# Heads of 64 rows against heads of 32 + 32 rows: the q and k layout of a dilated attention branch

## The chip, the cores and the metric

The kernel runs on one core of a Trainium2 chip. The metric is the time of one execution in microseconds on the device. Three runs of the kernel before gave 249.78, 249.79 and 250.01 us; the median is 249.79 us. The core has five engines that run side by side: TensorE (PE, matmuls; its weight loads are shown apart as PEld), VectorE (DVE), ScalarE (ACT), GpSimd (POOL) and SyncE (SP), and DMA queues.

## The reference, cut to what matters

Two layers run over 256 positions of width 1024. Each layer normalises its input, projects it by one large weight, runs three branches on the parts of the projection (dilated attention with 8 heads, a gated linear recurrence, stick-breaking attention with 4 heads), gates them, and projects back. Only the dilated branch is touched here.

```python
def apply_partial_rope(x, cos, sin):          # x: one head of 64; ROPE_DIM = 16
    x1, x2 = x[..., :8], x[..., 8:16]
    return concatenate([x1*c - x2*s, x2*c + x1*s, x[..., 16:]], -1)   # 48 of 64 are left as they are

qa, ka = rope(a_q), rope(a_k)                 # 8 heads of 64
s = einsum('bhqd,bhkd->bhqk', qa / 8, ka)     # with masks of three dilated windows
p = softmax(s); y = p @ v
```

Of a head's 64 numbers, 16 are rotated by a table of sines and cosines, and 48 pass. The scores of a head are one product over its 64 numbers.

## The kernel before, in words

All matrix work is exact fp32, either as three products of split numbers (high and low halves of the weights, `whi` and `wlo`, and of the activations, `xh` and `xl`), or as plain fp32 matmuls. ACT makes `whi` (line 109) and DVE makes `wlo` (line 110) for each chunk of weights that SP loads; up to four chunks are held.

The order of TensorE's instructions is written out by hand (`manual_schedule` for PE). The order on DVE and ACT is found by the framework's scheduler when the program is built, so an edit on these engines can move other instructions too.

`proj_b` (line 314) computes 256 columns of the projection, transposed: columns on the partitions, two blocks `b` of 128 columns, 256 positions each. The 256 columns of one chunk of q or k are four heads; a block holds two heads, 64 rows each. In layer 0 the result stays in one PSUM bank (`pp`), since it must still be scaled by a row `rb` of the normalisation; in layer 1 each block is added up by ACT (`low`, line 335) and DVE (line 337) into an SBUF tile.

`rotate` (lines 476 to 484) is four DVE instructions over 128 rows and both blocks, 512 columns each: a shuffle of rows (481), a product with the cosines (482; the table has ones in the 48 rows that pass), a product of the shuffled copy with the sines (483; zeros there), and a sum (484). In layer 0 the table `rp0` already carries the factor `rb` (line 596).

`dil_scores` (line 489) computes the scores of four heads. For two heads at a time it takes two PSUM banks (`s`, from a pool of four) and issues four matmuls (line 497) in the order: first 128 queries of head one, of head two, then the other 128 queries of each. Head one lies on rows 0 to 63 of the array, head two on rows 64 to 127. The trace shows each fp32 matmul as two records. DVE then adds the mask and takes the minimum (504), ACT takes the exponential, and TensorE transposes the result (463) for the product with the values (427).

There are four such score blocks: `second()` runs inside the projection of the second q chunk, `third()` inside the projection of the gate, in each of two layers. `rotate` is called eight times. `sb_scores` (443) has the same form as `dil_scores` and is not changed. `lru_gates` (557) uses 64 by 64 pieces of the array.

Of the kernel before, what the change touches and what calls it, by code (L numbers as in the profile page):

```python
# [13 lines left out]
ALU = mybir.AluOpType  # L14

P = 128
S = 256
# [3 lines left out]
NK = D // P  # L21
HD = 64
# [18 lines left out]
SHUF = list(range(8, 16)) + list(range(0, 8)) + list(range(16, 32))  # L41

CH_AV, CH_CV, CH_CQ, CH_CK, CH_BX, CH_CG, CH_BG, CH_AG, CH_O = 0, 2, 3, 4, 7, 10, 11, 12, 14
CH_AQ, CH_AK = (5, 8), (6, 9)
# [4 lines left out]
def trunk_kernel(ctx: ExitStack, tc: tile.TileContext, x, first_x, first, wpack, prm_d, gatew, gains, consts, rope, out):  # L49
    nc = tc.nc  # L50
    act, dve, pe, gps = nc.scalar, nc.vector, nc.tensor, nc.gpsimd
# [7 lines left out]
    at = ctx.enter_context(tc.tile_pool(name="at", bufs=4, space=bass.MemoryType.PSUM))  # L59
    yp = ctx.enter_context(tc.tile_pool(name="yp", bufs=1, space=bass.MemoryType.PSUM))  # L60

    def bank(pool, tag):
        return pool.tile([P, 512], F32, name=tag, tag=tag)

    def scr(w):
        return wk.tile([P, 512], F32, name="scr", tag="scr", bufs=SCR)[:, 0:w]
# [20 lines left out]
    def v2(a, n=2):  # L87
        return a.rearrange("p (b t) -> p b t", b=n)
# [28 lines left out]
    def ask(l, c, ahead=AHEAD):  # L117
        last = order.index((l, c)) + ahead
        while pending and order.index(pending[0]) <= last:
            i = pending.pop(0)  # L120
            ready[i] = load_chunk(*i)

    def weights(l, c, ahead=AHEAD):
        ask(l, c, ahead)
        return ready.pop((l, c))
# [16 lines left out]
    for k in range(NK):  # L142
# [24 lines left out]
        for (i, (a, b)), (ps, base, c0, c1) in seq:  # L167
            for t in range(NT):
                pe.matmul(ps[t][:, c0 - base:c1 - base], a[:, k, t * P:(t + 1) * P], b[:, c0:c1],  # L169
                          start=k == 0 and i == 0 and c0 == base, stop=k == NK - 1 and i == 2,  # L170
# [35 lines left out]
    def mm3(ps, lhs, rhs, ks, first, last):  # L206
        lh, ll = lhs
        rh, rl = rhs
        seq = [(a, b, k) for a, b in ((lh, rh), (lh, rl), (ll, rh)) for k in ks]
        for i, (a, b, k) in enumerate(seq):  # L210
            pe.matmul(ps, a(k), b(k), start=first and i == 0, stop=last and i == len(seq) - 1)  # L211
# [80 lines left out]
    rp = cst.tile([P, 2, S], F32, name="rp")  # L292
    rp0 = cst.tile([P, 2, S], F32, name="rp0")
    rb = cst.tile([P, S], F32, name="rb")
    gn = cst.tile([P, D], F32, name="gn", tag="gn")

    for l in range(L):
# [16 lines left out]
        def proj_b(c, mid=None, to=None, sc=1.0):  # L314
            pair = c in PAIRED[l]
            hi, lo = [a.rearrange("p (k c) -> p k c", c=256) for a in weights(l, c, AHEAD - 1 if mid else AHEAD)]
            if pair:
                flat = None if to is not None else scr(512)
                to = v2(flat) if to is None else to
            else:  # L320
                flat = bank(pp, "pp")
            for b in range(2):
                cs = slice(b * P, b * P + P)
                if pair:
                    ps = bank(pp, "pp")
                    seq = [(0, k) for k in range(NK - 1)] + [(1, k) for k in range(NK)] + [(0, NK - 1)]
                    for i, (is_lo, k) in enumerate(seq):
                        if is_lo:
                            pe.matmul(ps[:, 0:S], lo[:, k, cs], xh[:, k, :], start=False, stop=False,  # L329
                                      skip_group_check=True)  # L330
                        else:
                            pe.matmul(ps, hi[:, k, cs], xx[:, k].rearrange("p h t -> p (h t)"), start=i == 0,  # L332
                                      stop=i == len(seq) - 1, skip_group_check=True)
                    low = wk.tile([P, S], F32, name="low", tag="low", bufs=2)
                    act.activation(low, ps[:, S:2 * S], AF.Copy, scale=sc)  # L335
                    if sc == 1.0:
                        dve.tensor_add(to[:, b, :], ps[:, 0:S], low)
                    else:
                        dve.scalar_tensor_tensor(to[:, b, :], ps[:, 0:S], sc, low, ALU.mult, ALU.add)
                else:  # L340
                    mm3(flat[:, b * 256:(b + 1) * 256], [lambda k, a=a: a[:, k, cs] for a in (hi, lo)],
                        [lambda k, a=a: a[:, k, :] for a in (xh, xl)], range(NK), True, True)
                if b == 0 and mid:
                    mid()
                    ask(l, c)
            return flat

        def proj_to(dst, c, mid=None, sc=1.0):
            if l > 0 and c in PAIRED[l]:
                proj_b(c, mid, dst, sc)  # L350
            else:
                scaled(dst, proj_b(c, mid), sc)

# [30 lines left out]
        for t in range(NT):  # L384
            sc = rstd0[t] if l == 0 else 1.0
# [32 lines left out]
        def head(h):  # L418
            return slice((h % 2) * HD, (h % 2) * HD + HD), h // 2, slice(h * HD, (h + 1) * HD)
# [13 lines left out]
        zs, sw = {}, {}  # L433
        halves = ((0, slice(0, 128)), (1, slice(128, 384)))
# [38 lines left out]
            parts[2] = a[:, 768:1024], b[:, 0:128]  # L473
            return parts

        def rotate(ps, tiles, h0, tag):
            dst = tiles[h0] = sb.tile([P, 2, S], F32, name=tag, tag=tag)
            rt_ = rp0 if l == 0 else rp
            cc, ss = [rt_[:, i:i + 1, :].broadcast_to([P, 2, S]) for i in range(2)]
            sw = scr(512)  # L480
            dve.stream_shuffle(sw, ps, SHUF)
            dve.tensor_mul(dst, v2(ps), cc)
            dve.tensor_mul(v2(sw), v2(sw), ss)
            dve.tensor_add(dst, dst, v2(sw))

        qT, kT = {}, {}
        prob = {}

        def dil_scores(h0):
            sps = {}  # L490
            for p in (h0, h0 + 2):
                for h in (p, p + 1):
                    sps[h] = bank(at, "s")
                for t, cs in halves:
                    for h in (p, p + 1):
                        hr, hb, _ = head(h - h0)
                        pe.matmul(sps[h][:, cs], qT[h0][hr, hb, t * P:(t + 1) * P], kT[h0][hr, hb, 0:(t + 1) * P],  # L497
                                  start=True, stop=True)
            shifted = {}
            for h in range(h0, h0 + 4):  # L500
                xs = scr(384)
                mn = wk.tile([P, 2], F32, name="mn", tag="mn", bufs=4)
                for t, cs in halves:
                    dve.tensor_tensor_reduce(xs[:, cs], sps[h][:, cs], nmask[:, cs], -0.125, 3e38,  # L504
                                             ALU.add, ALU.min, mn[:, t:t + 1])
                shifted[h] = xs, mn
            return shifted
# [86 lines left out]
        if l == 0:  # L594
            for i in range(2):
                dve.tensor_mul(rp0[:, i, :], rp[:, i, :], rb)
        rotate(proj_b(CH_AQ[0], sb_scores), qT, 0, "q0")
        rotate(proj_b(CH_AK[0]), kT, 0, "k0")
        sw_t, sw_heads = turned_tile()
        conv(lambda: turned(sw, 0, (0,), sw_t))  # L600
        turned(sw, 0, (1, 2), sw_t)
# [3 lines left out]
            table(LN_EXP)  # L605
            dil_softmax(dil_scores(0))

        rotate(proj_b(CH_AQ[1], second), qT, 4, "q1")
        rotate(proj_b(CH_AK[1]), kT, 4, "k1")
        table(SIGM)  # L610
        cg_ps = proj_b(CH_CG)
        pts = dil_transposes(0)
# [15 lines left out]
        ps = proj_b(CH_AG)  # L628
# [26 lines left out]
        for t in range(NT):  # L655
# [3 lines left out]
            for n2 in range(2):  # L659
                cs = slice(n2 * 512, n2 * 512 + 512)  # L660
# [5 lines left out]
                for c0, c1 in parts:  # L666
                    c = slice(n2 * 512 + c0, n2 * 512 + c1)
# [19 lines left out]
def _rope_table():  # L687
    f = np.float32
    pos = np.arange(S, dtype=f)
    inv = f(500000.0) ** (-np.arange(0, 16, 2, dtype=f) / f(16))  # L690
    ang = (pos[:, None] * inv[None, :]).astype(f)
    cos, sin = np.cos(ang).T, np.sin(ang).T
    tab = np.zeros((P, 2, S), f)
    tab[:, 0] = 1.0
    for h in range(2):
        r = h * HD
        tab[r:r + 8, 0] = tab[r + 8:r + 16, 0] = cos
        tab[r:r + 8, 1] = -sin
        tab[r + 8:r + 16, 1] = sin
    return tab  # L700


def _pack_weights(w_in, w_out):
    wp = np.empty((L, NCH, P, 2048), np.float32)
    narrow = ((CH_CV, 3072), (CH_BX, 2048), (CH_BG, 2304), (CH_AG, 1536), (CH_AG + 1, 1792), (CH_CG, 3328),
              (CH_CQ, 2560), (CH_CK, 2816), (CH_AQ[0], 0), (CH_AQ[1], 256), (CH_AK[0], 512), (CH_AK[1], 768))
    yk = (4, 5, 6, 7, 0, 1, 2, 3)
    for l in range(L):
        wi = w_in[l].reshape(NK, P, 3584)
        for h in range(2):  # L710
            wp[l, CH_AV + h] = wi[4 * h:4 * h + 4, :, 1024:1536].transpose(1, 0, 2).reshape(P, 2048)
        for c, col in narrow:
            wp[l, c] = wi[:, :, col:col + 256].transpose(1, 0, 2).reshape(P, 2048)
        wo = w_out[l].reshape(NK, P, D)
        for h in range(2):
            for n in range(2):
                blk = np.stack([wo[k, :, n * 512:n * 512 + 512] for k in yk[4 * h:4 * h + 4]])
                wp[l, CH_O + 2 * h + n] = blk.transpose(1, 0, 2).reshape(P, 2048)
    return wp
# [56 lines left out]
```

## Time and profile before

| what | value |
|---|---|
| median of three runs | 249.79 us |
| the profiled execution | 248.82 us |
| its span, first to last instruction | 246.7 us |
| TensorE busy | 239.0 us, 97% |
| TensorE weight loads busy | 212.1 us, 86% |
| DVE busy | 196.5 us, 80% |
| ACT busy | 167.2 us, 68% |
| mean granted TensorE clock | 0.996 |

The profiled execution lies 0.97 us below the median of the runs; 2.1 us of it lie outside the span. Shares are means over the whole span; whether an engine that is 80% busy matters is read from who waits for it. Matmul records overlap, so the distance from one start to the next, not the length of a record, says what a matmul takes of TensorE's time.

### The profile page before, as it was taken

The page shows a single profiled execution, that of the slowest core. Times are in us where ns is not written, and L with a number is a line of the kernel's source. Part 1 is how long each engine was busy: PE and PEld are TensorE (multiplying, and loading weights), DVE is VectorE, ACT ScalarE, POOL GpSimd, SP SyncE. Part 2 cuts the span into 40 slices and gives each one's busy share as a digit, 9 for nine tenths or more (in the row PEclk, how much of TensorE's full clock was granted, in tenths as well). Part 3 has the DMA queues.
Part 4 walks back from the last instruction along what each step waited for, and adds up shares of the span by engine and source line. Part 5 has one row for each costly group of instructions (what it writes and reads, how often), then busy time and mean ns, then how long its engine had stood idle before and what let it go on. Part 6 is the DMA issues. An engine that isn't in the chain of part 4 may idle for free.

```text
span 246.7 us, 4531 instructions
## 1 busy us (share of the span) xinstructions
PE 239.0 (97%) x1657; PEld 212.1 (86%) x1657; DVE 196.5 (80%) x442; ACT 167.2 (68%) x360; POOL 12.1 (5%) x45
## 2 busy tenths in 40 slices
PE   8999999999999999999999999999999999999990
PEld 4889999999998899878889988889889889987870
DVE  3885699999999799985792766999999987985253
ACT  3778989735947499964662885865498649992142
POOL 0037000001000000000100000000010000000000
PEclk9999999999999999999999999999999999999998
DMA  6989889268447741277157486605553672000022
GB/s 201 404 292 403 342 288 333 96 215 268 134 157 255 258 117 56 85 240 284 74 189 232 142 268 243 200 7 165 161 157 119 197 262 98 0 0 3 0 85 85
DMA packets 13173, 43.89 MB, mean 178 GB/s; under 512 B 1632, under 2 KB 2144, under 8 KB 13152
## 3 DMA queue, kind: packets, MB, share of 16 engines
q1 hardware_dynamic: 12384, 42.30, 51.1%
q10 hardware_dynamic: 576, 0.79, 0.9%
q0 software_dynamic: 192, 0.52, 0.7%
q8 instruction: 13, 0.21, 0.4%
q14 instruction: 8, 0.07, 0.1%
HBM read 42.03 MB, written 1.05 MB: 175 GB/s over the span
## 4 chain that ended last, share of the span: by engine, by line
PE 94%; DMA 2%; DVE 1%; ACT 1%; SPq 0%; issue 0%; ACTq 0%
PE pp L211 51%; PE pp L332 11%; PE s L211 9%; PE pp L329 5%; PE s L169 4%; PE s L463 3%; PE s L497 2%; PE y L427 2%; DMA st<-first 2%; PE pp L169 2%; PE s L443 1%; PE pp L427 1%; PE s L557 1%; PE s L259 1%; DVE xres L668 0%; ACT scr L242 0%
## 5 line engine op out<-in xcount | busy, mean ns | idle before, releaser
L110 DVE TENSOR_TENSOR wlo<-st,whi 128x512 fp32r<-128x512 f32 x132 | 84.1, 683 | 12.8 <-ACT whi L109 12.5
L109 ACT ACTIVATE whi<-st 128x512 fp32r<-128x512 f32 x132 | 73.9, 629 | 28.0 <-PE pp L211 11.8
L211 PE MATMUL pp<-xx,whi 128*128 128x256 f32 x480 | 63.3, 285 | 0.0
L211 PEld LDWEIGHTS pp<-xx,whi 128*128 128x128 f32 x480 | 59.7, 191 | 1.4 <-issue 1.3
L211 PE MATMUL pp<-xx,wlo 128*128 128x256 f32 x240 | 33.7, 283 | 0.0
L211 PEld LDWEIGHTS pp<-xx,wlo 128*128 128x128 f32 x240 | 30.9, 192 | 0.0
L332 PE MATMUL pp<-xx,whi 128*128 128x512 f32 x112 | 29.3, 396 | 0.0
L332 PEld LDWEIGHTS pp<-xx,whi 128*128 128x128 f32 x112 | 20.1, 189 | 4.1 <-ACT scr L83 0.3
L77 ACT ACT_TABLE_LOAD x13 | 16.7, 1283 | 1.9 <-PEq L769 1.7
L83 ACT ACTIVATE pr<-scr,mn 128x128 f32<-128x128 f32 (+1 forms) x32 | 14.1, 442 | 5.2 <-DVE mn L504 5.2
L329 PEld LDWEIGHTS pp<-xx,wlo 128*128 128x128 f32 x112 | 15.3, 190 | 1.1
L329 PE MATMUL pp<-xx,wlo 128*128 128x256 f32 x112 | 15.6, 282 | 0.0
L211 PE MATMUL pp<-whi,yh 128*128 128x512 f32 x48 | 14.5, 403 | 0.0
L211 PE MATMUL pp<-wlo,yh 128*128 128x512 f32 x48 | 14.0, 393 | 0.0
L211 PE MATMUL pp<-whi,yl 128*128 128x512 f32 x48 | 14.0, 393 | 0.0
L335 ACT ACTIVATE low<-pp 128x256 f32<-128x256 f32 x14 | 5.3, 382 | 9.1 <-PE pp L332 6.8
L211 PEld LDWEIGHTS pp<-wlo,yh 128*128 128x128 f32 x48 | 9.0, 188 | 2.1
L211 PEld LDWEIGHTS pp<-whi,yl 128*128 128x128 f32 x48 | 9.0, 188 | 2.0
L211 PEld LDWEIGHTS pp<-whi,yh 128*128 128x128 f32 x48 | 8.6, 188 | 2.0 <-issue 0.3
L169 PE MATMUL s<-whi,xx 128*128 128x512 f32 (+1 forms) x36 | 10.2, 404 | 0.1
L415 ACT ACTIVATE yh<-scr 128x512 fp32r<-128x512 f32 x8 | 5.0, 631 | 7.7 <-DVE scr L413 7.6
L504 DVE CUSTOM_DVE_ANT_0 scr<-s,con 128x128 f32<-128x128 f32 (+1 forms) x32 | 9.2, 351 | 0.0
(165 smaller groups left out, 355.2 us busy)
## 6 DMA issues: line engine op xcount, KB each, us to landing
st<-w_pack SPq DMA_DIRECT2D x66, 512.0 KB, 5.4
st<-first SPq DMA_DIRECT2D x7, 512.0 KB, 6.2
xres<-x_in SPq DMA_DIRECT2D x2, 512.0 KB, 8.1
gw_t<-gate_w SPq DMA_DIRECT2D x2, 256.0 KB, 6.9
gn<-gains SPq DMA_DIRECT2D x1, 512.0 KB, 6.7
xs<-xc POOLq DMA_DIRECT2D x4, 128.0 KB, 3.7
gf<-gains SPq DMA_DIRECT2D x1, 512.0 KB, 6.8
out<-scr SPq DMA_DIRECT2D x2, 256.0 KB, 2.1
```

The lines of the kernel that those rows point to most:

```text
L77: load = act.preload_act_table_set(name)
L83: i = dep(act.activation(*a, **k), loaded["load"])
L109: split[l, c] = act.activation(hi[:, ws], st[:, ss], AF.Copy)
L110: dve.tensor_sub(lo[:, ws], st[:, ss], hi[:, ws].bitcast(F32))
L169: pe.matmul(ps[t][:, c0 - base:c1 - base], a[:, k, t * P:(t + 1) * P], b[:, c0:c1], start=k == 0 and i == 0 and c0 == base, stop=k == NK - ...
L211: pe.matmul(ps, a(k), b(k), start=first and i == 0, stop=last and i == len(seq) - 1)
L329: pe.matmul(ps[:, 0:S], lo[:, k, cs], xh[:, k, :], start=False, stop=False, skip_group_check=True)
L332: pe.matmul(ps, hi[:, k, cs], xx[:, k].rearrange("p h t -> p (h t)"), start=i == 0, stop=i == len(seq) - 1, skip_group_check=True)
L335: act.activation(low, ps[:, S:2 * S], AF.Copy, scale=sc)
L427: pe.matmul(y[hr, p * 128 + o:p * 128 + 256], vt[:, s0, hs], wts[i][s0], start=s0 == 0, stop=s0 == 1)
L463: pe.transpose(tp[:, i * P:(i + 1) * P], tiles[h0 + h][:, j * P:(j + 1) * P], ident)
L504: dve.tensor_tensor_reduce(xs[:, cs], sps[h][:, cs], nmask[:, cs], -0.125, 3e38, ALU.add, ALU.min, mn[:, t:t + 1])
```

## The change

The rows of q and k are laid out anew by the order of the weights' columns (`_pack_weights`): block 0 holds the first 32 numbers of each of four heads (the 16 that are rotated and 16 more), block 1 the other 32 of each. A head is then 32 rows of block 0 and the same 32 rows of block 1.

`rotate` becomes `rotated`. Shuffle, two products and the sum run over block 0 alone, 256 columns instead of 512. In layer 0 block 1 still needs its scale, a fifth instruction of 256 columns; in layer 1 the projection writes block 1 straight into the tile. In `dil_scores` all four banks are taken first, and each head's product over 64 rows becomes two products over 32 rows that accumulate in the bank: 16 matmuls in a block instead of 8, four heads in turn on four row groups.

```diff
-                to = v2(flat) if to is None else to
+                to = [v2(flat)[:, b, :] for b in range(2)] if to is None else to
...
-                        dve.tensor_add(to[:, b, :], ps[:, 0:S], low)
+                        dve.tensor_add(to[b], ps[:, 0:S], low)
...
-        def rotate(ps, tiles, h0, tag):
+        def rotated(c, tiles, h0, tag, mid=None):
             dst = tiles[h0] = sb.tile([P, 2, S], F32, name=tag, tag=tag)
-            rt_ = rp0 if l == 0 else rp
-            cc, ss = [rt_[:, i:i + 1, :].broadcast_to([P, 2, S]) for i in range(2)]
-            sw = scr(512)
-            dve.stream_shuffle(sw, ps, SHUF)
-            dve.tensor_mul(dst, v2(ps), cc)
-            dve.tensor_mul(v2(sw), v2(sw), ss)
-            dve.tensor_add(dst, dst, v2(sw))
+            tab_ = rp0 if l == 0 else rp
+            if l > 0:
+                src = scr(S)
+                proj_b(c, mid, [src, dst[:, 1, :]])
+            else:
+                ps = proj_b(c, mid)
+                src = ps[:, 0:S]
+            sh = scr(S)
+            dve.stream_shuffle(sh, src, SHUF)
+            dve.tensor_mul(dst[:, 0, :], src, tab_[:, 0, :])
+            dve.tensor_mul(sh, sh, tab_[:, 1, :])
+            dve.tensor_add(dst[:, 0, :], dst[:, 0, :], sh)
+            if l == 0:
+                dve.tensor_mul(dst[:, 1, :], ps[:, S:2 * S], rb)
...
         def dil_scores(h0):
             sps = {}
-            for p in (h0, h0 + 2):
-                for h in (p, p + 1):
-                    sps[h] = bank(at, "s")
-                for t, cs in halves:
-                    for h in (p, p + 1):
-                        hr, hb, _ = head(h - h0)
-                        pe.matmul(sps[h][:, cs], qT[h0][hr, hb, t * P:(t + 1) * P], kT[h0][hr, hb, 0:(t + 1) * P],
-                                  start=True, stop=True)
+            for h in range(h0, h0 + 4):
+                sps[h] = bank(at, "s")
+            for t, cs in halves:
+                for part in range(2):
+                    for h in range(h0, h0 + 4):
+                        hr = slice(32 * (h - h0), 32 * (h - h0) + 32)
+                        pe.matmul(sps[h][:, cs], qT[h0][hr, part, t * P:(t + 1) * P],
+                                  kT[h0][hr, part, 0:(t + 1) * P], start=part == 0, stop=part == 1)
...
-        rotate(proj_b(CH_AQ[0], sb_scores), qT, 0, "q0")
-        rotate(proj_b(CH_AK[0]), kT, 0, "k0")
+        rotated(CH_AQ[0], qT, 0, "q0", sb_scores)
+        rotated(CH_AK[0], kT, 0, "k0")
...
-    for h in range(2):
-        r = h * HD
+    for r in range(0, P, 32):
         tab[r:r + 8, 0] = tab[r + 8:r + 16, 0] = cos
...
-            wp[l, c] = wi[:, :, col:col + 256].transpose(1, 0, 2).reshape(P, 2048)
+            blk = wi[:, :, col:col + 256]
+            if c in CH_AQ + CH_AK:
+                blk = blk.reshape(NK, P, 4, 2, 32).transpose(0, 1, 3, 2, 4).reshape(NK, P, 256)
+            wp[l, c] = blk.transpose(1, 0, 2).reshape(P, 2048)
```

On TensorE, at the second score block of layer 0, the program before has these instructions (s is a PSUM bank, k1 and q1 the rotated tiles; the semaphores that an instruction waits for stand in brackets):

```order
L497 MATMUL s_1156<-k1_998,q1_929 128x128 [waits DVE_49,PE_49]
L497 MATMUL s_1157<-k1_998,q1_929 128x128 [waits PE_49]
L497 MATMUL s_1156<-k1_998,q1_929 128x256
L497 MATMUL s_1157<-k1_998,q1_929 128x256
L497 MATMUL s_1162<-k1_998,q1_929 128x128 [waits PE_49,Activation_49]
L497 MATMUL s_1163<-k1_998,q1_929 128x128 [waits PE_49,Activation_49]
L497 MATMUL s_1162<-k1_998,q1_929 128x256
L497 MATMUL s_1163<-k1_998,q1_929 128x256
```

In the changed program the block begins so, and goes on with eight of 128x256 that wait for nothing:

```order
L504 MATMUL s_1168<-k1_946,q1_811 128x128 [waits DVE_49,PE_49]
L504 MATMUL s_1169<-k1_946,q1_811 128x128 [waits PE_49]
L504 MATMUL s_1170<-k1_946,q1_811 128x128 [waits PE_49,Activation_49]
L504 MATMUL s_1171<-k1_946,q1_811 128x128 [waits PE_49,Activation_49]
L504 MATMUL s_1168<-k1_946,q1_811 128x128
L504 MATMUL s_1169<-k1_946,q1_811 128x128
L504 MATMUL s_1170<-k1_946,q1_811 128x128
L504 MATMUL s_1171<-k1_946,q1_811 128x128
```

The waits for the third and fourth bank, two of them on ACT, moved from the fifth and sixth matmul to the third and fourth. Before and after the block the neighbours on TensorE are the same.

On DVE, at the rotation of the first q and k chunk of layer 0 (pp is the projection's bank, rp_292 the scaled table, wlo a weight chunk's low half), the program before has:

```order
L481 STREAM_SHUFFLE scr<-pp 128x512
L482 TENSOR_TENSOR q_640<-pp,rp_292 128x512
L483 TENSOR_TENSOR scr<-scr,rp_292 128x512
L110 TENSOR_TENSOR wlo<-st,whi 128x512
L484 TENSOR_TENSOR q_640<-q_640,scr 128x512
L110 TENSOR_TENSOR wlo<-st,whi 128x512 x3
L481 STREAM_SHUFFLE scr<-pp 128x512
```

The changed program has in its place:

```order
L486 STREAM_SHUFFLE scr<-pp 128x256
L487 TENSOR_TENSOR q_528<-pp,rp_292 128x256
L488 TENSOR_TENSOR scr<-scr,rp_292 128x256
L491 TENSOR_TENSOR q_528<-pp,rb 128x256
L489 TENSOR_TENSOR q_528<-q_528,scr 128x256
L110 TENSOR_TENSOR wlo<-st,whi 128x512 x5
L486 STREAM_SHUFFLE scr<-pp 128x256
```

Four instructions of 512 columns became five of 256, and one more piece of `wlo` came ahead of the next shuffle.

## Rows read from the trace of the kernel before

**Rows 1.** The page: span, busy time by engine, busy tenths in 40 slices.
```profile
span 246.7 us, 4531 instructions
PE 239.0 (97%) x1657; PEld 212.1 (86%) x1657; DVE 196.5 (80%) x442; ACT 167.2 (68%) x360; POOL 12.1 (5%) x45
...
PE   8999999999999999999999999999999999999990
```

**Rows 2.** The page: the chain that ended last, by engine and by line.
```profile
PE 94%; DMA 2%; DVE 1%; ACT 1%; SPq 0%; issue 0%; ACTq 0%
PE pp L211 51%; PE pp L332 11%; PE s L211 9%; PE pp L329 5%; PE s L169 4%; PE s L463 3%; PE s L497 2%; PE y L427 2%; DMA st<-first 2%; PE pp L169 2%; PE s L443 1%; PE pp L427 1%; PE s L557 1%; PE s L259 1%; DVE xres L668 0%; ACT scr L242 0%
```

**Rows 3.** Waits of TensorE's weight loads, 24 to 240 us: total, times, longest.
```profile
PEld pp L211 <- issue: 1.7, 6, 0.3
...
PEld y L427 <- ACT whi L109: 0.4, 1, 0.4
PEld pp L332 <- ACT scr L83: 0.3, 1, 0.3
```

**Rows 4.** Chain of waits in order of time, the score blocks: start, us, what.
```profile
57.72 1.51 PE s L497 x16
...
81.78 1.51 PE s L497 x16
...
175.25 1.51 PE s L497 x16
...
199.06 1.51 PE s L497 x16
```

**Rows 5.** Timeline of TensorE inside the first score block, at four instants.
```profile
58.41 0.39 PE L497 MATMUL s<-k,q 64*128 64x128 f32 x4
...
58.51 0.50 PE L497 MATMUL s<-k,q 64*128 64x128 f32 x4
...
58.63 0.60 PE L497 MATMUL s<-k,q 64*128 64x256 f32 x4
...
58.84 0.38 PE L497 MATMUL s<-k,q 64*128 64x256 f32 x2
```

**Rows 6.** Timeline of TensorE in the gates' matmuls of layer 0.
```profile
78.21 0.38 PE L557 MATMUL s<-xc,gw_t 64*64 64x256 f32 x2
78.22 0.38 PE L557 MATMUL s<-xs,gw_t 64*64 64x256 f32 x2
78.42 0.38 PE L557 MATMUL s<-xc,gw_t 64*64 64x256 f32 x2
...
78.64 0.38 PE L557 MATMUL s<-xc,gw_t 64*64 64x256 f32 x2
```

**Rows 7.** Groups by line and shape: count, busy us, mean ns, idle before.
```profile
L497 PEld LDWEIGHTS s<-k,q 64*128 64x128 f32 x64 | 4.5, 187 | 0.9 <-issue 0.6
...
L483 DVE TENSOR_TENSOR scr<-scr,rp 128x512 f32<-128x512 f32 x8 | 5.5, 682 | 0.0
...
L596 DVE TENSOR_TENSOR rp<-rp,rb 128x256 f32<-128x256 f32 x2 | 0.7, 414 | 0.0
```

**Rows 8.** Timeline of DVE at the first rotation of layer 0.
```profile
45.54 0.68 DVE L482 TENSOR_TENSOR q<-pp,rp 128x512 f32<-128x512 f32 x1
46.13 0.68 DVE L483 TENSOR_TENSOR scr<-scr,rp 128x512 f32<-128x512 f32 x1
```

**Rows 9.** Busy time in two stretches: PE, PEld, DVE, ACT, POOL, clock, DMA.
```profile
44.00:75.00 31.00, 31.00 (x265) 30.49 (x264) 31.00 (x80) 19.26 (x43) 1.66 (x6) 1.00 0.56 177
160.00:194.00 34.00, 34.00 (x231) 30.65 (x230) 33.70 (x89) 24.61 (x58) 1.09 (x2) 1.00 0.38 121
```

**Rows 10.** Timeline of DVE and ACT: what the score blocks wait for.
```profile
80.02 0.86 ACT L83 ACTIVATE it<-s,prm_t 128x256 f32<-128x256 f32 x2
...
171.16 0.42 DVE L337 TENSOR_TENSOR bxp<-pp,low 128x256 f32<-128x256 f32 x1
171.49 0.68 DVE L484 TENSOR_TENSOR k<-k,scr 128x512 f32<-128x512 f32 x1
```

More of the change, by code (lines that the diff above doesn't have):

```diff
@@ L336, in proj_b @@
                     if sc == 1.0:
-                        dve.tensor_add(to[:, b, :], ps[:, 0:S], low)
+                        dve.tensor_add(to[b], ps[:, 0:S], low)
                     else:
-                        dve.scalar_tensor_tensor(to[:, b, :], ps[:, 0:S], sc, low, ALU.mult, ALU.add)
+                        dve.scalar_tensor_tensor(to[b], ps[:, 0:S], sc, low, ALU.mult, ALU.add)
                 else:
@@ L349, in proj_to @@
             if l > 0 and c in PAIRED[l]:
-                proj_b(c, mid, dst, sc)
+                proj_b(c, mid, [dst[:, b, :] for b in range(2)], sc)
             else:
@@ L606, in second @@
             dil_softmax(dil_scores(0))
-        rotate(proj_b(CH_AQ[1], second), qT, 4, "q1")
-        rotate(proj_b(CH_AK[1]), kT, 4, "k1")
+        rotated(CH_AQ[1], qT, 4, "q1", second)
+        rotated(CH_AK[1], kT, 4, "k1")
         table(SIGM)
```

## The prediction

> **What bounds the kernel now.** I read the page's busy line and slices first. TensorE is busy 97% of the span and full in all slices but the first and the last [rows 1]. A busy share can hide waits, since matmul records overlap, so the chain of waits comes next: 94% of the span is a chain of TensorE instructions that follow one another, DMA has 2% at the start, DVE 1% and ACT 1% in the tail [rows 2]. Third, the view of waits: between 24 and 240 us the matmuls wait for nothing, and the weight loads, which run one matmul ahead, have two short waits for ACT (0.4 and 0.3 us) and none for DVE; the longest entry, 1.7 us in six pieces, is put down to issue [rows 3]. So from the first layer's projections on, the time is the sum of what TensorE's own instructions take. DVE is as full as an engine can be where the rotations are (31.00 of 31 us, 33.70 of 34 us), and still TensorE does not wait for it there: it is busy for all 31 and all 34 us [rows 9]. The weights are split chunks ahead of their use, and that lead carries DVE's backlog.
>
> This leaves one place where the change can act on the time at once: the four score blocks, 1.51 us each, 6.04 us together, on the chain [rows 4].
>
> **The score blocks.** What does a block consist of? Eight matmuls are 16 records. Inside the first block the starts at 58.41 and 58.51 are 0.10 apart, the next at 58.63 is 0.12 on, the last at 58.84 is 0.21 on [rows 5]. Two records, one for each head, start together in such a slot. So a slot of 128 columns costs about 0.11 us, a slot of 256 about 0.215 us. Four of each are 4 x 0.11 + 4 x 0.215 = 1.30 us. The other 0.21 of 1.51 us is spent at the two ends, where TensorE goes from pieces of one form to another: before the second slot and after the last.
>
> After the change there are 16 matmuls, 32 records. If four heads share a slot as two did, 32 / 4 = 8 slots, again four of 128 and four of 256 columns: 1.30 us. Each record works on half the rows, but rows are not what a slot costs; columns are, and each slot has the same. The ends remain, since the block still stands between the same neighbours. What is added is the stagger in a slot. In the gates, four records on four pieces of the array run in one slot, the second pair 0.01 us behind the first, and the slots start at 78.21, 78.42 and 78.64, 0.21 to 0.22 us apart, as with two [rows 6]. Four to a slot is thus shown for 64 by 64 pieces at 256 columns; it is not shown for four row groups of 32 rows, nor for 128 columns. With that stagger a block ends 0.01 to 0.02 us later; four blocks add about 0.06 us.
>
> What the trace does not show is bounded from both sides. The best case is that one end vanishes: half of 0.21 us off each block, 4 x 0.1 = 0.4 us gained. On the other side, weight loads of 128 columns last 187 ns [rows 7] and follow one another every 0.11 us in a row group in the narrow slots. If only two row groups can be loaded at a time, the four narrow slots double, 4 x 0.11 = 0.44 us a block, 1.8 us in all, and the wide slots just hold two loads (2 x 0.11 = 0.22 us). If no more than two groups ever work together, all slots double: 4 x 1.30 = 5.2 us. I take +0.06 us, nearest to the gates' rows, which are of the same number type and in the same kernel.
>
> The gates show no loss from two to four pieces: 0.215 us a slot either way [rows 6]. The Trainium skill, page "TensorE: Matmul & The Clock Gate", section "Part 3: Packing small matmuls — row/col tiling", reports a speedup of 3.07 for four row tiles of 32 rows at 512 columns, not 4, and that speaks against the change: taken over as an estimate from that page, 1.30 x (4 / 3.07 - 1) = 0.39 us a block would be added, 1.6 us in all. No run here shows four row groups.
>
> **The waits of the score blocks.** The first four matmuls now want all four banks, where the third and fourth were wanted four matmuls later, some 0.6 us. In the second block of layer 0 the fourth bank is the gates' one, freed by ACT when its last sigmoid ends at 80.02 + 0.86 = 80.88 us [rows 10]; the block runs from 81.78 [rows 4]. That leaves 0.9 us, so nothing is late; behind these four stand the other 28 records and then the gate's projection, all in order on TensorE. Since the queue is filled ahead of the work, a wait that ends 0.9 us before may shorten that lead. If it does, I bound the loss at 0.6 us in that block, what the old order granted. In layer 1 ACT does the same work without a backlog. The tiles themselves are in time: the tightest, k of layer 1, is complete at 171.49 + 0.68 = 172.17 us, 3.1 us before its block [rows 4, 10], and the rotation gets shorter. I cost the waits at 0; the cover is ACT's lead and these 3.1 us.
>
> **The rotations.** Groups give 682 ns for 512 columns and 414 ns for 256 [rows 7], but instructions on DVE overlap, so starts say more: 45.54 to 46.13 is 0.59 us [rows 8], and a 256-column one gives way after 171.49 - 171.16 = 0.33 us [rows 10]. Before: 4 x 0.59 = 2.36 us a rotation. After, in layer 0: 5 x 0.33 = 1.65 us, 0.71 saved; in layer 1: 4 x 0.33 = 1.32 us, 1.04 saved. The shuffle at 256 columns is not in the trace; if it costs as before, 0.26 us a rotation less is saved. Four rotations in each layer: 4 x 0.71 + 4 x 1.04 = 7.0 us of DVE time, 3.6% of its 196.5. On the path to the end it is worth 0, because nothing on TensorE waits for DVE in those stretches; the weights' low halves are made earlier and then lie. ACT's instructions stay the same in number and size; the additions of layer 1 only change their target, and the masking that follows the scores still has many projections in between.
>
> **The sum**, against the profiled execution: 248.82 + 0.06 (score blocks) + 0 (waits) - 0 (rotations) = 248.88 us. The median of the runs lies 0.97 us above that execution, so the forecast is 249.85 us: no change.
>
> **Rivals.**
> Row groups do not go four abreast (slower). For it: no row shows four groups of 32 rows, and a slot of 128 columns has no more room than a weight load needs. Against it: the gates' four pieces. Its place is the four score blocks. It decides as soon as a narrow slot exceeds 0.11 us. Price: 1.8 us if the narrow slots double, 251.6 us; 5.2 us if all do, 255.0 us. Chance 0.15, mostly the lower price.
> The queue or the fourth bank holds the first group (slower). Twice as many instructions must reach TensorE in the same 1.5 us, and in layer 0 the sigmoid ends 0.9 us before. Up to 0.6 us in each of the two blocks that follow the values, 1.2 us in all, 250.4 to 251.0 us. Against it: the same stretch runs today without a wait. Chance 0.06.
> DVE's relief pays (faster). For it: DVE is full in both stretches. It could take away at most the two waits for ACT and half of the 1.7 us put down to issue, some 1.5 us, 248.3 us; or the ends of the blocks get shorter, 249.4 us. Against it: no wait for DVE in the list. Chance 0.05.
>
> **How the numbers follow.** The forecast has 0.74, and holds 249.4 to 250.3. I take 0.2%, 0.5 us, as what a measurement of this kernel can tell from no change. Faster by more: 0.05. Slower by more: the first rival, most of the second, 0.20. Within: 0.75. The range goes from 249.4 to 251.6 us, so that the doubled narrow slots are in it; it leaves out the case of all slots doubled and most of the gain.
>
> **What would show it.** Right: score blocks of about 1.53 us on the chain with 32 records; slots of four starts, 0.11 and 0.215 us apart; DVE's busy time lower by some 7 us or a little less; TensorE's share unchanged, and still no wait for DVE or ACT. Wrong: blocks of 1.9 us or more, or starts that come in pairs, mean the first rival; a wait of TensorE ahead of the second block of layer 0 means the second; blocks as before and a shorter span mean the third. A span that changes outside the score blocks by more than 0.5 us would refute the reading that TensorE's own sum is the time.

## The result and the profile after

Five runs of the changed kernel have a median of 251.01 us (250.2 to 251.73), five of the kernel before, on the same chip, 249.78 us. The ratio is 1.0049, with an interval from 1.0032 to 1.0065: the change makes the kernel slower by 1.23 us. That lies inside the range of 249.4 to 251.6 us, but the forecast was 249.85 us and no change, and the loss came from a step that had been costed at 0.

The profiled execution after took 251.73 us, 2.91 us more than the one before. Its page, as [rows 1]: span, busy time by engine, the slices of PE, then the shares of the chain.

```profile
span 249.6 us, 4669 instructions
...
PE 240.2 (96%) x1721; PEld 212.7 (85%) x1721; DVE 190.2 (76%) x446; ACT 167.0 (67%) x360; POOL 11.0 (4%) x45
...
PE   7899999998999999999999999999999999999990
...
PE 85%; DVE 6%; DMA 5%; ACT 1%; issue 1%; SPq 0%; DVEq 0%; ACTq 0%
```

DVE is busy 6.3 us less, as the step on the rotations said. But TensorE's tenth slice (56.2 to 62.4 us) has an 8 where [rows 1] have a 9, and the chain, which was TensorE for 94% [rows 2], now leaves it for DVE (6%) and DMA (5%). A chain that leaves the bounding engine in the middle of the program means that this engine waited there. The waits, from 24 to 242 us and with the columns of [rows 3], name the wait:

```profile
PE s L504 <- ACT wv L464: 0.9, 1, 0.9
...
PEld pp L211 <- issue: 1.7, 6, 0.3
...
PEld s L504 <- ACT wv L464: 1.2, 2, 1.0
```

Line 504 is the score matmul (497 before), line 464 ACT's eviction of the transposed stick-breaking weights `wv`. Neither kind of wait was there before. (One more name is new, `PEld pp L332 <- DVE xc L553`, 0.3 us; the same 0.3 us stood under issue before.) TensorE at the first block shows where it stood still:

```profile
58.70 0.49 PE L504 MATMUL s<-k,q 32*128 32x128 f32 x4
60.05 0.88 PE L504 MATMUL s<-k,q 32*128 32x128 f32 x6 [0.86 <-ACT wv L464]
```

The block's first records, on the first two banks, start at 58.70 us; the third bank's come at 60.05 us. The chain of the kernel after from 51.98 us on (start, us, what), and the three other score blocks, as [rows 4]:

```profile
51.98 0.41 DVE k L489
52.40 0.61 DVE wlo L110
...
53.02 5.84 DMA st<-w_pack
...
58.88 0.63 ACT whi L109
59.52 0.49 ACT wv L464
...
60.05 0.48 PE s L504 x2
...
60.54 1.57 PE s L504 x21
...
84.66 1.52 PE s L504 x32
...
178.13 1.52 PE s L504 x32
...
201.97 1.52 PE s L504 x32
```

The last three blocks have 32 records and last 1.52 us, against 1.51 us before: these are as forecast. The first block lost 1.8 us. Read backwards, its third and fourth bank waited for an eviction on ACT, this for a split `whi` that stands ahead of it, the split for weights that were issued at 53.02 and landed at 58.86 us, and their issue for the buffer that DVE's `wlo` set free at 53.01 us.

The time goes by stages of TensorE as follows, each from the start of one record to the start of another; "TensorE's end" is the start of its last record.

| stage | before, us | after, us |
|---|---|---|
| start of the span to the first weight chunk | 22.43 | 23.49 |
| first chunk to the first score block | 35.22 | 35.22 |
| first score block | 1.51 | 3.34 |
| its end to TensorE's end, with three score blocks | 180.76 | 180.79 |
| tail | 6.79 | 6.79 |

The first line is not the change: the first loads on the chain took 4.93 us in one execution and 6.12 in the other, before anything that the diff touches. Over the ten profiles of this case the line lies between 22.43 and 23.70 us: 22.43 to 23.31 with the old score blocks and 22.88 to 23.70 with the new ones. The rest is the first block, 1.81 us of wait and 0.012 for its longer records, and 0.03 us in the stage with the other three.

Why does ACT stand behind that split? ACT's timeline before (start, us, operation, count, idle before and what ended it):

```profile
53.34 1.15 ACT L109 ACTIVATE whi<-st 128x512 fp32r<-128x512 f32 x2 [3.91 <-DMA st<-w_pack]
54.40 0.58 ACT L464 ACTIVATE wv<-s 128x512 f32<-128x512 f32 x1
54.88 1.16 ACT L109 ACTIVATE whi<-st 128x512 fp32r<-128x512 f32 x2
55.94 1.06 ACT L464 ACTIVATE wv<-s 128x512 f32<-128x512 f32 x2
58.04 1.15 ACT L109 ACTIVATE whi<-st 128x512 fp32r<-128x512 f32 x2 [1.04 <-DMA st<-w_pack]
```

And after:

```profile
53.41 1.15 ACT L109 ACTIVATE whi<-st 128x512 fp32r<-128x512 f32 x2 [2.66 <-DMA st<-w_pack]
54.46 0.58 ACT L464 ACTIVATE wv<-s 128x512 f32<-128x512 f32 x1
56.14 1.15 ACT L109 ACTIVATE whi<-st 128x512 fp32r<-128x512 f32 x2 [1.09 <-DMA st<-w_pack]
58.88 0.63 ACT L109 ACTIVATE whi<-st 128x512 fp32r<-128x512 f32 x1 [1.59 <-DMA st<-w_pack]
59.42 1.06 ACT L464 ACTIVATE wv<-s 128x512 f32<-128x512 f32 x2
60.37 0.63 ACT L109 ACTIVATE whi<-st 128x512 fp32r<-128x512 f32 x1
```

Before, the two evictions stand ahead of the third split of this chunk (the gate's, `(0, CH_BG)` in the code) and end at 57.00 us, 0.7 us before the block. That split's weights were no earlier there: they landed at 58.02 us, 0.37 us behind the block's first record (57.65 us), against 0.16 us after the change. But nobody on TensorE waited for them yet. After, the third split stands ahead of the evictions. The transposes that these copy ended at 55.91 us (TensorE, line 463); ACT then stood idle for 1.59 us in front of the split and did not take the evictions first. The diff touches no instruction of ACT; the scheduler that lays out DVE and ACT changed their order.

### The profile page after: what moved, and what is told of

Its sections match the earlier page's. It is cut to its first block, busy times and chain, and to the rows that moved or that the text cites. A ratio compares the mean times of both kernels' runs of the same rounds, so it can differ in the third digit from the quotient of the medians.

```text
span 249.6 us, 4669 instructions
## 1 busy us (share of the span) xinstructions
PE 240.2 (96%) x1721; PEld 212.7 (85%) x1721; DVE 190.2 (76%) x446; ACT 167.0 (67%) x360; POOL 11.0 (4%) x45
## 4 chain that ended last, share of the span: by engine, by line
PE 85%; DVE 6%; DMA 5%; ACT 1%; issue 1%; SPq 0%; DVEq 0%; ACTq 0%
PE pp L211 44%; PE pp L332 11%; PE s L211 9%; PE pp L329 5%; PE s L169 4%; PE s L504 3%; PE s L463 3%; DMA st<-first 2%; DMA st<-w_pack 2%; PE y L427 2%; PE pp L169 2%; DVE sw L454 1%; DVE wlo L110 1%; PE pp L427 1%; PE s L443 1%; PE s L564 1%
## 5 line engine op out<-in xcount | busy, mean ns | idle before, releaser
L110 DVE TENSOR_TENSOR wlo<-st,whi 128x512 fp32r<-128x512 f32 x132 | 83.2, 683 | 12.7 <-ACT whi L109 12.4
L332 PE MATMUL pp<-xx,whi 128*128 128x512 f32 x112 | 29.3, 396 | 0.0
L332 PEld LDWEIGHTS pp<-xx,whi 128*128 128x128 f32 x112 | 20.1, 189 | 4.1 <-ACT scr L83 0.3
```

The lines of the kernel that those rows point to most:

```text
L110: dve.tensor_sub(lo[:, ws], st[:, ss], hi[:, ws].bitcast(F32))
```

## The experiments

Theory A: the order of ACT in this one place is the whole cost, and four row groups go abreast at no price. Rivals: the blocks themselves cost (B), the early want of all four banks is to blame whatever ACT's order is (C), DVE's relief is worth something in another place (D). Two sets of runs were made, each with its own runs of the kernel before, 249.47 us in the first (23 runs) and 249.71 us in the second (34).

**The evictions put first.** The changed kernel, with all splits of the chunk behind the last eviction.

```diff
                 split[l, c] = act.activation(hi[:, ws], st[:, ss], AF.Copy)
+                if (l, c) == (0, CH_BG):
+                    dep(split[l, c], evicted[0, 2])
...
-                act.activation(to[g], tp, AF.Copy)
+                evicted[l, g] = act.activation(to[g], tp, AF.Copy)
```

> The changed kernel, with one more edge for the scheduler: on ACT the first split of the gate's weight chunk (0, 11) stands behind the two evictions of the transposed stick-breaking weights. Theory (ACT's order: these evictions stand behind a split that waits for a weight DMA, so the first score block of layer 0 gets its third and fourth bank 1.36 us late): the wait goes, the block takes 1.52 us, time back to 249.8 us (249.5 to 250.1), and the spread of the runs shrinks from 1.5 us to under 0.5 us. Rival 1 (four row groups cost TensorE time): 251.0 us stays. Rival 2 (wanting four banks at once is the price): part of the wait stays, 250.4 us or more. Rival 3 (the first DMAs landed 1.2 us later): 251.0 us stays.

Measured: 249.91 us, ratio 1.0019 (1.0005 to 1.0032). No wait of the score matmuls for ACT is left, and the first block on the chain is

```profile
58.28 1.52 PE s L506 x32
```

Most of the loss is gone with the wait. The spread was wider than expected, 249.43 to 251.22 us. What is left, some 0.2%, leaves room for B, and this edit also delays two splits that were in time. In the profiled execution, 249.43 us, nothing of it is to be seen; it was the fastest of the twelve.

**Two heads at a time.** The same, with the 16 matmuls issued pair by pair.

```diff
-            for t, cs in halves:
-                for part in range(2):
-                    for h in range(h0, h0 + 4):
+            for p in (h0, h0 + 2):
+                for t, cs in halves:
+                    for part in range(2):
+                        for h in (p, p + 1):
```

> As the run before, but the 16 matmuls of a score block go pair by pair: first all of heads one and two, then all of heads three and four, so that no more than two row groups of 32 rows can work in a slot. Theory (four go abreast in the changed kernel, a slot costs by its columns): 16 slots in place of 8, 1.30 us more a block, 4 x 1.30 = 5.2 us, 255.0 us, blocks of 2.8 us. Rival 1 (four row groups never went abreast, or only in part): little or nothing is added, 249.8 to 252 us.

Measured: 251.83 us, ratio 1.0077 (1.0059 to 1.0094). TensorE in the second block of this kernel, at three instants (start, us, operation, records):

```profile
83.52 0.39 PE L507 MATMUL s<-k,q 32*128 32x128 f32 x4
...
83.74 0.60 PE L507 MATMUL s<-k,q 32*128 32x256 f32 x8
...
83.96 0.60 PE L507 MATMUL s<-k,q 32*128 32x256 f32 x10
```

A block lasts 2.07 us, 0.55 more than with four heads in turn, and 4 x 0.55 = 2.2 us agrees, within their spread, with the 1.9 us between the medians of this and the kernel above. So abreast matters, and B's way to pay is real. But the size was missed, 2.07 us and not 2.8: the second pair's records began beside the first pair's wide slots (eight records at 83.74 us, where two heads have four). The first pair's four narrow slots ran alone, for 0.55 us, and that is what the block grew by.

**The kernel before, with ACT in the changed order.**

```diff
+                evicted[l, g] = act.activation(to[g], tp, AF.Copy)
+                if tiles is sw and l == 0 and g > 0:
+                    dep(evicted[l, g], held["third"])
...
         turned(sw, 0, (1, 2), sw_t)
+        if l == 0:
+            dep(held["fourth"](), evicted[0, 2])
```

> The kernel before, its scores and rotations untouched, with ACT's order of the changed kernel forced on it: the two evictions stand behind the third split of the gate's weight chunk, the fourth split behind them. Theory: the same late banks; the old scores want them one pair later, some 0.65 us, so the first block of layer 0 waits 0.7 us and the time is 250.4 to 250.6 us. Rival 2 (the early want of four banks is the whole cause): 249.8 us. Rival 1: 249.8 us.

Measured: 251.12 us, ratio 1.0058 (1.004 to 1.0076). (The diff is cut; the rest keeps the two splits in `held` and puts the chunk's load a little earlier in the program. Counted from the first block's first record, the load was issued 4.15 us ahead, as in the kernel before, 4.16.) The chain is that of the kernel after, with the old matmuls on 64 rows (509 is their line here, 474 the eviction's):

```profile
54.38 3.95 DMA st<-w_pack
...
58.34 0.63 ACT whi L111
58.98 0.49 ACT wv L474
59.47 0.04 issue
59.51 0.48 PE s L509 x2
...
60.00 0.92 PE s L509 x4
```

The first block waits 0.81 us (0.7 expected), the others last 1.51 us. This order, in a kernel without the change, makes it slower by about as much as the change did. The median is 0.5 to 0.7 us above what was expected. The profiled execution took 250.49 us, 0.63 us less than the median; the wait depends on when one load lands, so this one profile does not say what the others waited.

**Less of the rotation.** The kernel before, without the product with the sines and the sum (this part of the computation is left out).

```diff
-            dve.tensor_mul(v2(sw), v2(sw), ss)
-            dve.tensor_add(dst, dst, v2(sw))
```

> The kernel before without the product with the sines and the sum in the rotation (that part of the computation is left out): DVE is relieved by about 8 x 1.2 = 9.6 us, the scores are untouched. Built, its ACT order at the evictions is that of the changed kernel. Theory: DVE's time is off the path, and the relief alone moves ACT's order; the first block of layer 0 waits some 0.7 us, 250.4 us. Rival (DVE's relief pays): 249.3 us or less. If neither: 249.8 us.

Measured: 249.81 us, ratio 1.0005 (0.9993 to 1.0017). ACT's timeline ahead of the first block:

```profile
54.72 1.79 ACT L109 ACTIVATE whi<-st 128x512 fp32r<-128x512 f32 x3 [1.34 <-PE s L463]
56.41 1.07 ACT L464 ACTIVATE wv<-s 128x512 f32<-128x512 f32 x2
```

DVE is busy 187.5 us, 9.0 less than [rows 1], and the time is the same: D falls. ACT has the changed order here too, three splits and then the evictions, so a shorter rotation, without the new layout, is enough to bring it about. Still nothing waited: the third split's weights were issued at 50.32 and landed at 55.85 us, and the evictions ended at 57.48 us, before the block at 58.18 us. The order alone, then, costs nothing; it costs when the load that the third split waits for is late. The expectation that the order decides by itself was wrong.

**ACT in the old order.** The changed kernel, with the dependency for the chunk's second half alone, so that ACT's instructions stand exactly as in the kernel before.

```diff
+                if (l, c, i) == (0, CH_BG, 1):
+                    dep(split[l, c], evicted[0, 2])
...
-                act.activation(to[g], tp, AF.Copy)
+                evicted[l, g] = act.activation(to[g], tp, AF.Copy)
```

> The changed kernel with only the third and fourth split of the gate's weight chunk put behind the two evictions: ACT's order at this place is then that of the kernel before, piece by piece; scores, rotations and DVE's order stay as changed. Theory (late evictions behind a split that waits for a weight DMA): no wait before the first score block, blocks of 1.52 us, time as before, ratio 1.000 to 1.001. Rival (the new scores or the DVE order cost by themselves): ratio 1.003 or more.

Measured: 249.67 us, ratio 0.9994 (0.9981 to 1.0007). ACT's timeline:

```profile
55.16 1.15 ACT L109 ACTIVATE whi<-st 128x512 fp32r<-128x512 f32 x2 [1.11 <-PE s L465]
56.22 1.06 ACT L466 ACTIVATE wv<-s 128x512 f32<-128x512 f32 x2
57.92 1.15 ACT L109 ACTIVATE whi<-st 128x512 fp32r<-128x512 f32 x2 [0.64 <-DMA st<-w_pack]
```

Here the change is whole, and it costs nothing: the last load still came after the evictions' end, but behind them. The first block lasts 1.52 us on the chain. From its start to TensorE's end this kernel takes 0.05 us more than the one before, the four blocks' longer records. B falls to that.

**The changed kernel again**, as it is, beside the one above.

> The changed kernel once more, on the same chip as the others of this call. Theory: first score block of 3.0 to 3.4 us, ratio 1.004 to 1.007.

Measured: 251.34 us, ratio 1.0064 (1.0043 to 1.0085), 1.67 us above the kernel above. The load landed at 58.13 us here, and the wait was 1.32 us. The chain:

```profile
52.79 5.34 DMA st<-w_pack
...
59.32 0.48 PE s L504 x2
```

The runs lie between 249.88 and 253.45 us, a wider spread than any other kernel's here. That a wait which hangs on one late load inherits the load's variation would explain it, and the two profiles bear this out: counted from the block's first record the load landed 0.16 us late in the first (58.86 against 58.70 us) and 0.34 us early here (58.13 against 58.47 us), 0.50 us apart, and the waits are 0.49 us apart. The other runs have no trace. In the kernel above the load landed just as here, 0.34 us ahead of the block (57.90 against 58.24 us), and nothing waited: between these two profiles ACT's order alone makes 1.32 us.

**The load brought forward.** The changed kernel with ACT's order left alone; the low halves that free the load's buffer go ahead of k's first rotation on DVE.

```diff
+            first = (l, c) == (0, CH_AK[0])
+            if first:
+                ask(l, CH_BX)
-            dve.stream_shuffle(sh, src, SHUF)
+            turn_rows = dve.stream_shuffle(sh, src, SHUF)
+            if first:
+                dep(turn_rows, low_of[0, CH_AK[1], 0, 512])
```

> The changed kernel with ACT's order as changed (the evictions stay behind the third split), but on DVE the low halves of chunk (0, 9) are made ahead of the rotation of the first k. The load buffer that the third split's DMA needs is then free some 1.7 us earlier. Theory (the wait ends with that DMA): it lands 1.7 us earlier, the wait before the first score block shrinks from 1.8 to 0.1 to 0.4 us, ratio 1.000 to 1.002, although k is rotated 1.8 us later. Rival (ACT's order costs by itself, whatever lands when): the wait stays at 1.8 us, ratio 1.005.

Measured: 250.15 us, ratio 1.0015 (1.0004 to 1.0027). The load was issued at 51.57 and landed at 57.24 us. ACT's timeline:

```profile
57.27 0.63 ACT L109 ACTIVATE whi<-st 128x512 fp32r<-128x512 f32 x1
57.80 1.07 ACT L464 ACTIVATE wv<-s 128x512 f32<-128x512 f32 x2
```

The evictions end at 58.87 us, 0.1 us before the block at 58.99 us, and nothing waits. A load that lands 1.3 to 1.8 us earlier than in the two profiles of the changed kernel, each counted from its block's first record, takes away most of the loss with the bad order in place. The 0.4 us left in the median may be executions in which the load lands later, since there is so little room; only one has a trace. That one took 250.15 us, as the median, and the wait has no part in its excess: its first loads took 6.34 us, against 5.65 in the profiled execution of the kernel with ACT in the old order (249.51 us).

**The early want alone.** The kernel before, all four banks taken first, halves outside and pairs inside.

```diff
-            for p in (h0, h0 + 2):
-                for h in (p, p + 1):
-                    sps[h] = bank(at, "s")
-                for t, cs in halves:
+            for h in range(h0, h0 + 4):
+                sps[h] = bank(at, "s")
+            for t, cs in halves:
+                for p in (h0, h0 + 2):
```

> The kernel before, its 64-row heads and rotations untouched, but all four banks are taken first and the first halves of all four heads go before the second halves. ACT's order at the evictions is that of the kernel before. Theory: early want alone costs nothing, since the evictions end 0.6 us before the block: ratio 1.000. Rival (the early want is the price): 1.003 or more.

Measured: 249.67 us, ratio 0.9995 (0.9985 to 1.0005), and the first block on the chain as in [rows 4]:

```profile
58.46 1.51 PE s L497 x16
```

C falls as a cause by itself. With the evictions late it adds to the wait, and the traces give its share. The table has, for each profile, when the third split's load landed, counted from the first record of the first block (minus: ahead of it), and how much longer that block lasted than the others.

| kernel | ACT's order | load landed, us | wait, us |
|---|---|---|---|
| before | evictions first | +0.37 | 0 |
| before, early want alone | evictions first | -0.26 | 0 |
| before, ACT in the changed order | split first | -0.21 | 0.81 |
| before, less of the rotation | split first | -2.26 | 0 |
| after | split first | +0.16 | 1.81 |
| after, again | split first | -0.34 | 1.32 |
| after, ACT in the old order | evictions first | -0.34 | 0 |
| after, load brought forward | split first | -1.68 | 0 |

With the split first, the changed kernel's wait is the landing plus 1.65 us, and none where that is below 0, as with the load brought forward. A landing at -0.21 us would make it wait some 1.44 us, by this estimate from its two profiles; the old matmuls waited 0.81. So the early want adds about 0.6 us where the evictions are late, which is what the old order granted the third and fourth bank, and nothing where they are in time.

Theory A holds, then, in another form: the cost is ACT's order together with a late load, and the early want makes it larger.

No version is faster than the kernel before by more than the noise. TensorE's own sum is the time, and the change does not shorten it.

## Why the prediction was right or wrong, step by step

The measured median lies in the range, and that is luck. The range went up to 251.6 us so that doubled narrow slots would be in it, and these did not come; a wait that had been costed at 0 filled the same room. The point forecast of no change failed: the result is in the part called slower, which had a chance of 0.20.

**What bounds the kernel** was right. Outside the first block TensorE's stages agree to 0.03 us between the two programs, but for the start, and 6.3 or 9.0 us less on DVE gained nothing.

**The score blocks** were right in count and size. Eight slots were forecast; here are the starts in the second block of the kernel after, at four instants, to be read against [rows 5]:

```profile
84.80 0.40 PE L504 MATMUL s<-k,q 32*128 32x128 f32 x8
...
84.91 0.40 PE L504 MATMUL s<-k,q 32*128 32x128 f32 x8
...
85.02 0.51 PE L504 MATMUL s<-k,q 32*128 32x128 f32 x8
...
85.13 0.60 PE L504 MATMUL s<-k,q 32*128 32x256 f32 x6
```

Slots follow one another every 0.11 us, as with two heads, and eight records where there were four run at one instant (two slots overlap). A block grew by 0.012 us; 0.01 to 0.02 had been forecast. The first rival, with most of the chance on the slower side, is out: weight loads of 185 ns on four row groups go every 0.11 us.

The Trainium skill, page "TensorE: Matmul & The Clock Gate", section "Part 3: Packing small matmuls — row/col tiling", has 3.07 for four row tiles at 512 columns, and the estimate from it was 0.39 us a block. The trace does not agree for this form: 1.52 us against 1.51, one hundredth and not four tenths.

**The waits of the score blocks**, costed at 0 with "the cover is ACT's lead and these 3.1 us", is the step that failed: the term measured 1.81 and 1.32 us in the two profiles. It looked at the second block of layer 0, where the sigmoid frees the fourth bank 0.9 us ahead [rows 10], and at k in layer 1; there nothing waited, as forecast. The first block's third and fourth bank were not looked at: evictions of `wv` free them, 0.7 us ahead in the trace of before, less than in the place that was examined. And the cover was taken from the old order of ACT. "ACT's instructions stay the same in number and size" is true, 360 of them before and after, but not in order. In ACT's order of the two programs the place reads, before and then after (`wv` are the evictions, `whi` the splits):

```
L109 ACTIVATE whi<-st 128x512 x2
L464 ACTIVATE wv<-s 128x512 x2
L109 ACTIVATE whi<-st 128x512 x2
```

```
L109 ACTIVATE whi<-st 128x512 x3
L464 ACTIVATE wv<-s 128x512 x2
L109 ACTIVATE whi<-st 128x512
```

This can be read from the programs before either runs, and the trace of before bounds its price: the third split started at 58.04 us, after a wait for its load. Put ahead of the evictions it takes 0.53 us (half of 54.88 to 55.94 us, two splits), they end at 58.04 + 0.53 + 1.06 = 59.63 us, and the fourth bank, wanted as the block starts at 57.72 us, is late by 1.9 us.

**The rotations** were right, at 0 for the gain and in their size. Summed over their lines the rotations' instructions take 22.3 us before and 15.2 us after, 7.1 us less where 7.0 was forecast; all other DVE instructions add up to 204.0 us in both. DVE's busy time, which counts overlapping instructions once, fell by 6.3 us. The shuffle of 256 columns, which no row of before had, gives back as much as the products do, 40% of its duration:

```profile
L481 DVE STREAM_SHUFFLE scr<-pp 128x512 f32<-128x512 f32 x4 | 3.0, 743 | 0.0
...
L486 DVE STREAM_SHUFFLE scr<-pp 128x256 f32<-128x256 f32 x4 | 1.8, 448 | 0.0
```

(columns as in [rows 7], before and after; the product goes from 682 to 412 ns). "The weights' low halves are made earlier and then lie" was half the story: the scheduler used the room for another order, on DVE with five pieces ahead of k's rotation where there were four, and on ACT with three splits ahead of the evictions. The run with less rotation shows that the shorter work on DVE is enough for this, and that the order costs only together with a late load. By what rule the scheduler came to it was not examined.

**The rivals.** The second had the mechanism, a bank that holds the first group, but in the second block and for at most 0.6 us, the room of the old order on TensorE. The price was ACT's queue, not TensorE's: an eviction that stands behind a load waits as long as the load does. That its 250.4 to 251.0 us end where the median lies is luck as well. The third did not come.

## What to carry to other kernels

Where a scheduler orders an engine's instructions and the engine takes them in that order, as ACT did here, compare the order of every engine, also of those whose instructions the diff does not touch, and look ahead of each instruction that frees something for the bounding engine: does a transfer now stand between? A cover of less than a microsecond is a term to be recomputed from the new order, not a zero. When such a wait is found, pin the one pair of instructions by a dependency and see the change by itself; here that took the ratio from 1.0064 to 0.9994.

## What the runs showed of the hardware

Four groups of 32 rows take fp32 matmuls at the pace of two groups of 64, 0.11 us for 128 columns. The groups are not in lockstep, nor in the program's order among each other: with the heads issued in pairs, all matmuls of the first pair stand ahead of the second pair's in the program, but the second pair's first records start 0.56 us into the block, between wide ones of the first pair at 0.55 and 0.77 us. So a block lasted 2.07 us rather than the 2.8 of strict pairs. The first loads of an execution took between 4.93 and 6.34 us in the ten profiles, which by itself moves the span by more than a microsecond; stages counted from the first weight chunk are free of it.
